# A hybrid encoder step on one core: squares turned by VectorE, an output projection two tiles ahead, and a sync queue in source order

## The chip, the core and the metric

The kernel runs on one core of one Trainium2 chip, in one launch. The metric is the device time of an execution in microseconds. Engines are named as the profile names them: PE is TensorE (PEld its weight loads), DVE is VectorE, ACT is ScalarE, POOL is GpSimd; SPq and ACTq are the instruction queues of SyncE and ScalarE that issue transfers.

## What is computed

One step of a two-layer encoder over 2048 prompt rows and 32 sampled rows of width 1024, all in float32. The first layer is a gated delta rule with 8 heads of 128; the second is a sliding-window attention with 16 query heads of 64, 4 key heads and a sink in each softmax. Both end in an output projection, a residual and a layer norm.

```python
def delta_layer(x, conv_buf, s0, w_in, conv_w, a_log, dt_bias, norm_w, w_out, ln_g, ln_b):
    proj = x @ w_in
    qkv, new_buf = causal_conv(proj[..., :CONV_DIM], conv_buf, conv_w)
    z = proj[..., CONV_DIM:CONV_DIM + A_VW].reshape(b, l, A_HEADS, A_DV)
    ...
    q = l2norm(qkv[..., :A_QK].reshape(b, l, A_HEADS, A_DK)) * (A_DK ** -0.5)
    k = l2norm(qkv[..., A_QK:2 * A_QK].reshape(b, l, A_HEADS, A_DK))
    v = qkv[..., 2 * A_QK:].reshape(b, l, A_HEADS, A_DV).astype(jnp.float32)
    ...
    o, s_new = gated_delta_rule(q, k, v, g, beta, s0.astype(jnp.float32))
    o = o * lax.rsqrt(jnp.mean(o * o, -1, keepdims=True) + RMS_EPS) * norm_w * jax.nn.silu(z.astype(jnp.float32))
    out = o.reshape(b, l, A_VW).astype(x.dtype) @ w_out
    return layer_norm(DN_ALPHA * x + out, ln_g, ln_b), new_buf, s_new.astype(x.dtype)
```

Behind it stand the shared key and value projection (`shared_kv`, a rotary turn on 16 of the 64 key dimensions) and the attention layer (`swa_layer`: own query and gate projections, banded softmax over 192 keys, output projection, layer norm). Outputs are y of all rows, the two states, the convolution rows and the last keys and values.

## The kernel before, in words

Every float32 product is split into a high and a low part and made of three products in a faster type, accumulated in PSUM. Five parts follow one another, with some overlap; intermediate tensors go through scratch in HBM.

**Projections (class P1, 0 to about 735 us).** Activations of all 2080 rows stay in SBUF in five blocks of 416. For each of 24 heads of q, k and v (indices 0 to 23), a row R of 128 channels by 2080 tokens is made by 5 x 24 products (`project`, lines 74 to 83). `conv` (line 199) then runs four taps, a tanh and a gate on it, and stores y, channels on partitions, to scratch in pieces of 512 bytes (lines 217 to 220). For q and k it squares y into the single buffer th on ScalarE, turns the squares in 32 x 32 squares on VectorE (line 225) and sums them for the norms. From head 15 on (`ordered`, line 232) the order of every engine is written by hand, with the decay matrices (`decays`) between. `split_out_weights` splits the output weights in 16 steps, one a head for heads 6 to 14, the others later. Then come 8 heads of the gate z.

**Delta rule (class Delta, about 710 to 1132 us).** 17 chunks: the 32 sampled rows first (chunk 0), then 16 of 128 rows. `ORDER` (line 613) is one list of steps with offsets: in iteration i the step `gq1+2` runs for chunk i+2, and so on, so that several chunks are under way at once. The list is the order of PE, DVE and ACT; the sync queue is ordered by a planner, which estimates when each transfer can start. Steps that matter here: `tk` and `tv` transpose keys and values on TensorE against the identity (`turn`, line 815), ScalarE scales the results out of PSUM (`kd`, `vn`; line 825), `fk` fades k in place after its transposes have been read, `Lk`, `Lv`, `Lq`, `Lz`, `Lgb`, `LE` are loads. k has two buffers. Up to iteration 10 the last gate products (`GA0` to `GA3`, class LateGate) fill TensorE; from iteration 11 the first layer's output weights are loaded in 16 steps. The sampled chunk makes its o early, but its gate and store come in `first_end` (line 1012), called at the last chunk's step `OSC`; `done` marks a chunk as stored.

**Output projection (classes OutNorm and O1).** 17 tiles in the order of their rows, the 32 sampled ones last. `O1.tiles` (line 1238) is a generator. In the last two iterations of the delta rule each TensorE step gives it 0.45 us of work (line 1003), afterwards it runs alone. For a tile it loads the gated o (g, one buffer) and the residual rows r one tile ahead, splits g in high and low parts, makes 2 x 24 products of 512 columns, adds them to r (line 1134), takes mean and variance and norms r in four half-row steps on VectorE (lines 1203 and 1205). `turned` (line 1224) then transposes the normed tile on TensorE, eight squares through PSUM, and stores it as hT. Between tiles `more` brings work of the next part: block 0 of hT (`load0`), and sums of blocks for a fast matrix product (`presum`, on GpSimd, stored from the sync queue, line 1376).

**Second layer's projections (class P2, about 1310 to 1735 us)** make keys, values, queries and gates, with seven products in place of eight for pairs of blocks (Strassen's scheme). `turn` (line 1710) transposes values on TensorE through one PSUM bank and two copies on ScalarE. `out_weights` splits the second layer's output weights beside it.

**Attention (class Attention, to the end)** isn't touched.

## Time and profile before

| | us |
|---|---|
| runs | 2104.82, 2105.94, 2102.75; median 2104.82 |
| profiled execution | 2110.58 |
| its span, first to last instruction | 2108.8 |
| mean granted TensorE clock | 0.989 |
| busy: PE, DVE, ACT, POOL | 2048.6, 1468.9, 989.0, 911.0 |

The span is what the traces below are measured in; the execution's own time has 1.8 us around it. A table of stretches gives for each engine the busy time and the number of instructions, then the granted clock, the mean share of the 16 transfer engines that were busy, and the bytes that they moved. A row of a timeline gives start, length, engine, line, operation and tiles, and in brackets how long the engine had stood idle and what ended that. A row of the groups by line gives count, busy time, mean length in ns, and idle time before.

### The profile page before, as it was taken

To read this page: it belongs to the slowest core of one execution; us is meant where nothing else is said; L and a number is where in the kernel's file an instruction comes from. 1 tells how busy PE (TensorE), PEld (TensorE's weight loads), DVE (VectorE), ACT (ScalarE), POOL (GpSimd) and SP (SyncE) were. 2 spreads that over 40 slices of the span, in tenths; PEclk is the share of its full clock that TensorE was granted. 3 is DMA by queue.
4 is the path that set the end of the run, shared out by engine and by line. 5 is a ranking of instruction groups with operands and counts; after the bars stand their busy time and mean duration, and the time that the engine had idled before them with its cause. 6 is when DMAs were issued, how large, how long until landed. Compare 5 with 4: busy or idle time off the path is not lost.

```text
span 2108.8 us, 37301 instructions
## 1 busy us (share of the span) xinstructions
PE 2048.6 (97%) x13694; PEld 1875.4 (89%) x13694; DVE 1468.9 (70%) x2587; ACT 989.0 (47%) x2465; POOL 911.0 (43%) x1248
## 2 busy tenths in 40 slices
PE   7999999999999999999999999999999999999998
PEld 5999999999999999999887887889989997777775
DVE  4476666675647678888887887768877755566565
ACT  4354444446532267777762211534644445455552
POOL 0322223212222177778752112157436515566666
PEclk9999999999999999999999999999999999999999
DMA  5132333236665545455766666778776659533421
GB/s 206 33 90 88 97 110 111 82 102 226 193 185 179 182 137 179 159 169 182 271 209 227 212 213 219 254 229 296 243 240 222 226 171 317 127 101 107 114 72 66
DMA packets 292763, 360.85 MB, mean 171 GB/s; under 512 B 74260, under 2 KB 217460, under 8 KB 292564
## 3 DMA queue, kind: packets, MB, share of 16 engines
q1 hardware_dynamic: 278576, 334.29, 49.9%
q10 hardware_dynamic: 14004, 24.17, 3.6%
q8 instruction: 108, 1.77, 0.3%
q14 instruction: 75, 0.61, 0.1%
HBM read 235.54 MB, written 134.06 MB: 175 GB/s over the span
## 4 chain that ended last, share of the span: by engine, by line
PE 83%; DMA 7%; DVE 3%; POOL 3%; issue 2%; ACT 1%; SPq 0%; ACTq 0%; DVEq 0%; POOLq 0%
PE ps L79 12%; PE ps L81 11%; PE ps L80 11%; PE ot L1126 3%; PE ot L1127 3%; PE ot L1128 3%; PE S L1992 2%; PE po L1126 2%; PE ot L2025 2%; PE po L1128 2%; PE po L1127 2%; PE tr L2007 2%; PE X L1653 2%; PE X L1651 2%; PE X L1652 2%
## 5 line engine op out<-in xcount | busy, mean ns | idle before, releaser
L79 PE MATMUL ps<-act_hi,w_hi 128*128 128x416 f32 x1280 | 454.9, 355 | 0.0
L81 PE MATMUL ps<-act_hi,w_lo 128*128 128x416 f32 x1280 | 450.2, 352 | 0.0
L80 PE MATMUL ps<-act_lo,w_hi 128*128 128x416 f32 x1280 | 447.9, 350 | 0.0
L79 PEld LDWEIGHTS ps<-act_hi,w_hi 128*128 128x128 f32 x1280 | 240.3, 188 | 3.8 <-issue 0.4
L80 PEld LDWEIGHTS ps<-act_lo,w_hi 128*128 128x128 f32 x1280 | 240.6, 188 | 3.0
L81 PEld LDWEIGHTS ps<-act_hi,w_lo 128*128 128x128 f32 x1280 | 240.1, 188 | 3.3
L209 DVE SCALAR_TENSOR_TENSOR y<-R,convw,y 128x2083 f32<-128x2083 f32 x72 | 182.5, 2536 | 60.9 <-ACT y L206 44.9
L56 POOL TENSOR_TENSOR w_lo<-w_raw,w_hi 128x1024 fp32r<-128x1024 f32 x25 | 71.4, 2858 | 330.9 <-ACT w_hi L55 303.6
L729 POOL TENSOR_TENSOR tm<-L,Tt 128x60 f32<-128x60 f32 (+19 forms) x365 | 132.5, 363 | 84.8 <-issue 39.9
L1826 POOL TENSOR_TENSOR P<-e,sm 128x384 f32<-128x384 f32 (+2 forms) x128 | 102.3, 820 | 118.0 <-DVE sm L1816 111.6
L731 POOL TENSOR_TENSOR Tt<-Tt,tm 128x60 f32<-128x60 f32 (+19 forms) x365 | 139.8, 383 | 28.6
L1812 ACT ACTIVATE e<-S,nm 128x193 f32<-128x193 f32 (+2 forms) x260 | 104.6, 415 | 97.3 <-DVE nm L1807 56.5
L1330 DVE TENSOR_TENSOR w_lo<-w_raw,w_hi 128x512 fp32r<-128x512 f32 x132 | 136.7, 1053 | 18.5 <-ACT w_hi L1342 12.7
L1126 PE MATMUL po<-wo_hi,g_hi 128*128 128x512 f32 x256 | 104.9, 410 | 8.1 <-DVE r L1134 7.9
L305 ACT COPY R<-ps 128x416 f32<-128x416 f32 (+1 forms) x144 | 60.4, 442 | 109.3 <-PE ps L81 95.8
L1482 ACT ACTIVATE o<-X 128x416 f32<-128x416 f32 x80 | 41.4, 518 | 134.7 <-PE X L1653 134.6
L1126 PE MATMUL ot<-wo,g_hi 128*128 128x512 f32 x256 | 103.6, 405 | 0.0
L1128 PE MATMUL po<-wo_hi,g_lo 128*128 128x512 f32 x256 | 101.2, 396 | 0.5 <-DVE g_lo L1169 0.5
L1127 PE MATMUL po<-wo_lo,g_hi 128*128 128x512 f32 x256 | 101.1, 395 | 0.0
L1127 PE MATMUL ot<-wo,g_hi 128*128 128x512 f32 x256 | 100.8, 394 | 0.0
L1128 PE MATMUL ot<-wo,g_lo 128*128 128x512 f32 x256 | 100.8, 394 | 0.0
L1342 ACT CAST w_hi<-w_raw 128x512 fp32r<-128x512 f32 x129 | 76.8, 616 | 21.5 <-PE ps L1652 6.7
(362 smaller groups left out, 5119.4 us busy)
## 6 DMA issues: line engine op xcount, KB each, us to landing
w_raw<-in_b_w SPq DMA_DIRECT2D x60, 512.0 KB
w_raw<-in_w_in SPq DMA_DIRECT2D x40, 512.0 KB
act_raw<-s_hT SPq DMA_DIRECT2D x64, 208.0 KB
s_rows<-o SPq DMA_DIRECT2D x50, 208.0 KB
k<-s_k SPq DMA_DIRECT2D x17, 512.0 KB
E<-s_E SPq DMA_DIRECT2D x17, 512.0 KB
s_bq<-s_rows SPq DMA_DIRECT2D x40, 208.0 KB
s_bz<-o SPq DMA_DIRECT2D x40, 208.0 KB
```

Source lines behind the costliest of these rows:

```text
L79: nc.tensor.matmul(ps, hi[:, k, :], xh[:, k, :], start=(k == 0), stop=False)
L80: nc.tensor.matmul(ps, hi[:, k, :], xl[:, k, :], start=False, stop=False)
L81: nc.tensor.matmul(ps, lo[:, k, :], xh[:, k, :], start=False, stop=(k == KC - 1))
L209: nc.vector.scalar_tensor_tensor(out=y[:], in0=R[:, j:j + W], scalar=self.convw[:, i, j:j + 1], in1=y[:], op0=ALU.mult, op1=ALU.add)
L729: P.tensor_tensor(out=tm[:n, i0 - k:, :w], in0=L[:n, i0:, j:j + 1].to_broadcast(sh), in1=Tt[:n, j:j + 1, :w].to_broadcast(sh), op=ALU.mult)
L731: P.tensor_tensor(out=Tt[:n, i0:, :w], in0=Tt[:n, i0:, :w], in1=tm[:n, i0 - k:, :w], op=ALU.subtract)
L1126: nc.tensor.matmul(ps[:n], ghi[:, k, :n], hi, start=a, stop=False)
L1127: nc.tensor.matmul(ps[:n], ghi[:, k, :n], lo, start=False, stop=False)
L1128: nc.tensor.matmul(ps[:n], glo[:, k, :n], hi, start=False, stop=z)
L1330: P.tensor_tensor(out=lo, in0=raw, in1=hi, op=ALU.subtract)
L1812: self.nc.scalar.activation(x.e[:, h, u, :x.n], x.S[:, h, u, :], AF.Exp, bias=x.nm[:, h, u:u + 1], scale=1.0, accum_out=x.sm[:, h, u:u + 1])
L1826: self.nc.gpsimd.tensor_tensor(out=x.P[:, u, :nj * 128].rearrange("r (j h k) -> r j h k", h=2, k=64), in0=x.e[:, :, u, :n].rearrange("r h ...
```

## The change

It does four things.

- Keys and values are turned in the first stage. For k and v, VectorE turns y itself in 32 x 32 squares; for k the squares are taken afterwards, so the number of turns is the same, and for v they are added. `by_token` stores the turned tile to scratch with tokens on rows, in pieces of 32 floats, four transfers a head for the prompt and four for the sampled rows. The delta rule loads them so (`Lt`, `Lv`) and ScalarE scales them in place; `tk` and `tv` go. The loads have new places in `ORDER`.
- The output projection's normed rows and the second layer's values are turned by VectorE in squares too, and stored in pieces of 32 floats.
- `O1.tiles` is rewritten: g comes two tiles ahead, the norm of a tile ends during the next one (a scaling on ScalarE, two full-row products and a turn on VectorE), the sampled tile is first and waits for its gate, which is made after the last chunk's store. `load0` and the presums are spread over tiles, and the presums are stored from ScalarE's queue.
- The sync queue takes the source order in the delta rule, and in the projection ScalarE and the sync queue do.

Besides, the first layer's output weights are split at heads 1 to 6, and the second layer's begin eight steps later.

```diff
@@ P1.qkv
-            if 6 <= i < self.FREE:
+            if 1 <= i < 7:
                 next(self.wo)
@@ P1.conv
+        if kind < 2:
+            dst = T["qk"[kind]]
...
+        pieces = (th[:, 0:NP], y[:, 0:NP]), (th[:, NP:NT], y[:, NP + 3:NP + 3 + NS])
+        if kind == 0:
+            for a, b in pieces:
+                nc.scalar.activation(a, b, AF.Square)
+            nc.vector.transpose(R[:, 0:NT], th[:, 0:NT])
+        else:
+            for a, b in pieces:
+                nc.vector.transpose(a, b)
+            self.by_token(T[("kt", "v")[kind - 1]], h, th)
+            if kind == 2:
+                return
+            yield
+            nc.scalar.activation(R[:, 0:NT], th[:, 0:NT], AF.Square)
...
+    def by_token(self, dst, h, turned):
+        for a in range(4):
+            s = slice(32 * a, 32 * a + 32)
+            self.nc.sync.dma_start(dst[0:NTT - 1, :, h, s].rearrange("t (b i) j -> i (t b) j", i=32),
+                                   turned[s, 0:NP].rearrange("i (b j) -> i b j", j=32))
+            self.nc.sync.dma_start(dst[NTT - 1, 0:NS, h, s], turned[s, NP:NT])
@@ Delta
-        ta2+0 fq1+1 os0+0 v5+0 Lk+2 PC2+1 OSC+-1 Lq1+2 PC3+1 fq0+1 vn0+1 G0+2 u3+0 N0+2 G1+2 TT+2 otr0+-1
...
+        at0+2 o1+0 y1+1 ks0+1 e0+1 U32+1 ks1+1 Lk+3 v2+1 v3+1 GA2+1 gth+0 sq1+0 Lv0+2 Lv1+2 WL+1 X+0
+        Lz1+0 Lq0+3 ta1+1 v4+1 gz1+0 GA0+2 u1+1 e1+1 R+0 gz2+0
...
+    def by_token(self, ch, q, src, dst):
+        t = self.four.tile([128, 4, 128], F32, tag=dst, name=dst)
+        ch.__dict__.setdefault(dst, {})[q] = t
+        self.nc.sync.dma_start(t[:ch.n], self.T[src][ch.ti, :ch.n, q * 4:q * 4 + 4, :])
...
-    def turn(self, ch, x, name):
-        tr = self.bank(self.pa, ch, name)
-        for j in range(4):
-            self.nc.tensor.transpose(tr[:ch.n, j, :], x[:, j, :ch.n], self.G["ident"][:, :])
...
                     if c == last and name == "OSC":
-                        self.first_end(chunks[0], second, done)
+                        second.give(5.5)
                     if name == "st1":
                         done(chunks[c])
+                        if c == last:
+                            self.first_end(chunks[0], done)
+                            second.give(1.5)
@@ OutNorm
+    def scaled(self, r, n):
...
+        V.tensor_scalar(out=nb[:n], in0=mv[:n, 0:1], scalar1=rs[:n, 0:1], scalar2=-1.0, op0=ALU.mult, op1=ALU.mult)
+        nc.scalar.activation(r[:n], r[:n], AF.Identity, bias=nb[:n, 0:1], scale=rs[:n, 0:1])
+
+    def affine(self, r, n):
+        V, tabs = self.nc.vector, self.tabs
+        V.tensor_tensor(out=r[:n], in0=r[:n], in1=tabs[0][:n], op=ALU.mult)
+        V.tensor_tensor(out=r[:n], in0=r[:n], in1=tabs[1][:n], op=ALU.add)
@@ O1.turned
+        hT = self.room().rearrange("p a b -> p (a b)")
+        self.nc.vector.transpose(hT[:n], h[:n])
+        self.nc.sync.dma_start(self.T["h"][row:row + n, :], h[:n])
+        rows = self.T["hT"].rearrange("h (c j) t -> j (h c) t", j=32)
+        for a in range(0, n, 32):
+            self.nc.sync.dma_start(rows[:, :, c0 + a:c0 + a + 32],
+                                   hT[a:a + 32].rearrange("j (c i) -> j c i", i=32))
@@ O1.tiles
+        on, last, parts, beside = self.on, None, [], ()
+        for t in tiles[:2]:
+            while not ready(t):
+                yield 1.0
+            g = self.fetch(*t)
+            yield 0.0
+            parts.append(on.low(g, on.cast(g, t[2]), t[2]))
         r = self.rows(*tiles[0])
         for i, t in enumerate(tiles):
+            beside, coming = itertools.chain(beside, more(i)), tiles[i + 2:i + 3]
+            if i + 1 == len(tiles):
+                yield from (out for out in beside if out)
+            for j, out in enumerate(on.tile(parts.pop(0), r, t[2])):
+                yield out
+                if j == 0:
+                    for c in coming:
+                        while not ready(c):
+                            yield 1.0
+                        g = self.fetch(*c)
+                next(beside, None)
+                if j == 1 and last:
+                    on.affine(*last)
+                    self.turned(last[0], *tiles[i - 1])
+                if j == 3 and i + 1 < len(tiles):
+                    following = self.rows(*tiles[i + 1])
+            for c in coming:
+                high = on.cast(g, c[2])
+            on.scaled(r, t[2])
+            for c in coming:
+                parts.append(on.low(g, high, c[2]))
+            last, r = (r, t[2]), following
+        on.affine(*last)
+        self.turned(last[0], *tiles[-1])
+        yield from more(len(tiles))
@@ P2.out_weights
+        for _ in range(8):
+            yield
@@ P2.turn
+        nc, t = self.nc, self.out()
+        nc.vector.transpose(t[:], c[:])
...
+        for a in range(4):
+            self.delay(lambda a=a: store(a), 1 + a)
@@ program
-        tiles = [(t * 128, t * 128, min(128, NT - t * 128)) for t in range(NTT)]
+        tiles = [(t * 128, t * 128, min(128, NT - t * 128)) for t in (NTT - 1, *range(NTT - 1))]
         yield from o1[0].tiles(tiles, lambda t: t[0] in sent, more)
 
     def more(i):
+        if 6 <= i < 10:
+            yield from p2[0].load0(2 * i - 12)
+        elif 12 <= i < 16:
+            for _ in range(4 if i < 15 else 0):
+                next(p2[0].main)
+            yield from p2[0].presum(0, p2[0].raw_act, 2, (i - 12,), nc.scalar, 3)
+        elif i == 16:
+            yield from p2[0].go(4)
+        elif i == 17:
+            yield from p2[0].go(8)
...
-    with tc.manual_schedule(engines={ET.PE, ET.DVE, ET.Activation}):
+    with tc.manual_schedule(engines={ET.PE, ET.DVE, ET.Activation, ET.SP}):
         delta.run(chunks, S, LateGate(p1, zp, w, raw), second, side, done)
...
-    with tc.manual_schedule(engines={ET.PE}):
-        with tc.manual_schedule(engines={ET.DVE}):
-            second.rest()
+    with tc.manual_schedule(engines={ET.PE, ET.DVE, ET.Activation, ET.SP}):
+        second.rest()
```

## Rows read from the trace of the kernel before

**Rows 1.** The page's first part: busy time, share of the span and instructions.

```profile
PE 2048.6 (97%) x13694; PEld 1875.4 (89%) x13694; DVE 1468.9 (70%) x2587; ACT 989.0 (47%) x2465; POOL 911.0 (43%) x1248
```

**Rows 2.** Busy time of each engine by stretch of the span.

```profile
core 0: us, PE busy (x) PEld busy (x) DVE busy (x) ACT busy (x) POOL busy (x), PEclk, DMA share, GB/s
...
250.00:430.00 180.00, 180.00 (x958) 178.36 (x957) 119.37 (x50) 76.77 (x94) 43.83 (x46) 1.00 0.32 100
...
735.00:980.00 245.00, 245.00 (x2760) 233.13 (x2759) 202.34 (x486) 172.33 (x556) 185.80 (x496) 0.99 0.49 162
980.00:1081.00 101.00, 92.98 (x1184) 89.32 (x1182) 89.96 (x245) 74.19 (x252) 78.58 (x221) 0.98 0.73 246
...
1132.00:1332.00 200.00, 192.10 (x906) 158.09 (x904) 157.12 (x337) 33.71 (x50) 41.91 (x35) 0.98 0.67 218
1332.00:1735.00 403.00, 389.19 (x2023) 378.29 (x2022) 294.46 (x375) 187.97 (x380) 196.65 (x127) 0.97 0.73 237
```

**Rows 3.** Groups by line, engine PE: the transposes; count, busy us, mean ns, idle.

```profile
L818 PE MATMUL vtr<-ident,v 128*128 128x128 f32 (+1 forms) x136 | 21.8, 283 | 0.0
...
L1232 PE MATMUL ps<-ident,r 128*128 128x128 f32 (+1 forms) x132 | 19.4, 269 | 0.2 <-ACT o L1439 0.2
...
L818 PE MATMUL ktr<-ident,k 128*128 128x128 f32 (+1 forms) x136 | 17.9, 274 | 0.2 <-DVE npr L702 0.2
...
L1714 PE MATMUL tp<-ident,o 128*104 128x128 f32 x40 | 7.0, 303 | 3.2 <-ACT o L1718 3.2
```

**Rows 4.** Timeline of PE in the steady delta rule.

```profile
836.28 1.03 PE L818 MATMUL ktr<-ident,k 128*128 128x128 f32 x8
837.15 1.06 PE L846 MATMUL vp<-vn,u 128*128 128x128 f32 x8
```

**Rows 5.** The chain that ended last: start us, us, what; pieces of chunks, two loads.

```profile
846.65 1.09 PE gq L831 x8
...
870.44 1.09 PE gq L831 x8
...
965.59 1.09 PE gq L831 x8
...
1011.67 6.43 DMA k<-s_k
...
1074.52 1.09 PE gq L831 x8
...
1249.93 2.44 DMA act_raw<-s_hT
```

**Rows 6.** Waits of PE and DVE: us in total, times, longest us.

```profile
PE po L1126 <- DVE r L1134: 7.9, 3, 3.8
...
PE tp L1714 <- ACT o L1718: 3.2, 2, 3.0
...
DVE k L841 <- PE ktr L818: 13.5, 13, 1.4
```

**Rows 7.** Timeline of DVE in the output projection.

```profile
1208.29 0.69 DVE L1234 COPY hT<-ps 128x512 f32<-128x512 f32 x1 [1.91 <-PE ps L1232]
...
1215.66 1.22 DVE L1169 TENSOR_TENSOR g_lo<-g,g_hi 128x1024 fp32r<-128x1024 f32 x1
...
1220.12 0.69 DVE L1234 COPY hT<-ps 128x512 f32<-128x512 f32 x1 [1.91 <-PE ps L1232]
```

**Rows 8.** Line 225, DVE: the turn of squares; ns min, median, max.

```profile
L225 DVE STREAM_TRANSPOSE R<-th x16: 2285/2345/2346, 98.9 to 421.9; 128x2080 f32<-128x2080 f32 x16
```

**Rows 9.** Groups of PE from 1081 to 1132 us: the projection's products.

```profile
L1126 PE MATMUL po<-wo_hi,g_hi 128*128 128x512 f32 x32 | 13.6, 426 | 0.2 <-ACT g_hi L1168 0.2
```

**Rows 10.** Stretches with stores of 512-byte pieces, then 128-byte pieces; columns as [rows 2].

```profile
262.30:266.20 3.90, 3.90 (x22) 3.87 (x22) 2.29 (x1) 2.01 (x3) 0.00 (x0) 1.00 0.98 273
...
1334.10:1334.90 0.80, 0.80 (x6) 0.78 (x5) 0.69 (x2) 0.00 (x0) 0.00 (x0) 1.00 1.11 174
```

More of the change, by code (lines that the diff above doesn't have):

```diff
@@ L1015, in first_end @@
         self.load(c0, "z")
-        second.give(5.5)
         for q in range(2):
@@ L1021, in first_end @@
         done(c0)
-        second.give(1.5)
     def sampled(self, pool):
@@ L1179, in tile @@
             cs = slice(c * 512, c * 512 + 512)
[L1180 removed]
+            ps = self.bank(c)
             for k in range(KC):
@@ L1213, in __init__ @@
         self.on = OutNorm(tc, es, "o1", "left", I, "a", 2, T["wo"])
-        self.bank = lambda: self.on.pp.tile([128, 512], F32, tag="po", name="tr")
-        self.steps = 0
-        self.room = lambda: self.on.one.tile([128, KC, 128], F32, tag="g", name="hT")
+        self.steps, self.room = 0, None
     def fetch(self, c0, row, n):
@@ L1253, in tiles @@
-            while not all(ready(u) for u in tiles[i + 1:i + 2]):
-                yield 1.0
-            ahead = self.fetch(*tiles[i + 1]) if i + 1 < len(tiles) else None
-            following = self.rows(*tiles[i + 1]) if i + 1 < len(tiles) else None
-            self.on.queue = self.nc.sync if i < 9 else self.nc.scalar
-            for j, out in enumerate(self.on.tile(got, r, t[2], True)):
-                if isinstance(out, float):
-                    yield out
-                    if j == 3 and ahead is not None:
-                        ahead = self.on.split(ahead, tiles[i + 1][2])
-                    if j >= 6:
-                        yield from itertools.islice(late, 1)
@@ L1265, in tiles @@
-            self.nc.sync.dma_start(self.T["h"][t[1]:t[1] + t[2], :], out[:t[2]])
-            late = self.turned(out, *t)
-            got, r = ahead, following
-            if i + 2 == len(tiles):
-                yield from more(1)
-        yield from more(2)
-        yield from late
+            beside, coming = itertools.chain(beside, more(i)), tiles[i + 2:i + 3]
[14 more added lines that the diff above has]
+                    following = self.rows(*tiles[i + 1])
@@ L1359, in take_act, with presum @@
         return t
-    def presum(self, pair, load, pace, slices=range(4)):
+    def presum(self, pair, load, pace, slices=range(4), queue=None, hold=0):
         c, d = self.PAIRS[pair]
@@ L1374, in presum @@
                     yield
+            for _ in range(hold):
+                yield
             for n, t in (("t1", b11), ("t3", b12), ("t2", b22), ("t4", b21)):
-                self.nc.sync.dma_start(T["sums"][pair, int(n[1]) - 1, k], t[:])
+                (queue or self.nc.sync).dma_start(T["sums"][pair, int(n[1]) - 1, k], t[:])
                 for _ in range(pace // 4):
@@ L1710, in turn, with store @@
     def turn(self, c, half, b):
[L1711 to L1719 removed]
+        nc, t = self.nc, self.out()
+        nc.vector.transpose(t[:], c[:])
+        rows = self.T["bv"][b * TB:(b + 1) * TB, half * 128:half * 128 + 128]
+        rows = rows.rearrange("(b i) (a j) -> a i b j", i=32, j=32)
+        def store(a):
+            s = slice(32 * a, 32 * a + 32)
+            nc.sync.dma_start(rows[a], t[s].rearrange("i (b j) -> i b j", j=32))
+        for a in range(4):
+            self.delay(lambda a=a: store(a), 1 + a)
 class Attention:
@@ L2283, in side @@
             o1.append(O1(tc, left, I, O, T, G))
+            o1[0].room = lambda: delta.four.tile([128, KC, 128], F32, tag="k", name="hT", bufs=Delta.BUFS)[:]
         else:
```

153 lines of the change are left out of this document (53 added, 100 removed).

## The prediction, made before the changed kernel ran

> **What bounds the kernel now.** I read the shares of busy time first, then the table by stage, then the groups of TensorE, then timelines and chain. TensorE is busy 97% of the span [rows 1]; the reader should see that it is the only engine near full. The table by stage [rows 2] shows where: it has no gap in the projections (250 to 430 us) and in the steady part of the delta rule (735 to 980), with VectorE at 202.3 of 245 us there. It has gaps where the delta rule runs without gate products (980 to 1081: 93.0 of 101), in the output projection (1132 to 1332: 192.1 of 200) and in the second layer's projections (1332 to 1735: 389.2 of 403). So in the gapless stretches a TensorE instruction that goes is time that goes; in the others I have to look for what ends the gap.
>
> **The transposes on TensorE.** There are 136 + 136 for keys and values, 136 of the normed rows (132 and a group of 4) and 40 of the second layer's values [rows 3]. Their durations of some 270 ns overlap; the price is start to start: eight key transposes begin at 836.28 and the next product at 837.15, so 0.87 us, 0.109 us each [rows 4]. All 448 are 48.8 us if TensorE bounds everywhere. It doesn't, so part by part:
>
> *Delta rule, steady.* A full chunk has 16 transposes, 16 x 0.109 = 1.74 us. The period is 870.44 - 846.65 = 23.79 us [rows 5], without a gap; it would be 22.05. VectorE needs 202.3/245 x 23.79 = 19.6 us of it and fits. VectorE also loses its wait for the key transposes before the fading of k, 13.5 us over 13 chunks [rows 6]; ScalarE scales as many tiles as before, from loaded tiles. I take 1.6 of the 1.74 us for ten chunks: **16 us** (ends: 0 and 17).
>
> *Delta rule, last chunks.* From 965.59 to 1074.52 five periods take 21.8 us each [rows 5], with TensorE idle; VectorE is busy 90.0 of 101 us [rows 2], 19.4 us a period, and the load of k holds the chain for 6.43 us [rows 5]. The change issues that load in the iteration before, once its buffer is free. VectorE then sets the period; with 1 us of waits that stay I take 20.4, so 5 x 1.4 = **7 us** (ends: 2, and 5 x 1.74 = 9). The first two chunks give **2 us**.
>
> *Output projection, steady.* A tile takes 1220.12 - 1208.29 = 11.83 us [rows 7], with 8 transposes, 0.87 us. On VectorE goes a copy (0.69) and four half-row steps of about that (2.8); to it come two full-row products at 1.22 (the full-row subtraction in the same rows) and one turn of 1024 columns, half of 2.345 us for 2080 [rows 8], 1.15: 3.6 against 3.5 us. It waited 1.91 us a tile for the transposes [rows 7], so it fits into 10.96 us. Saved: 136 x 0.109 = 14.8 us, and TensorE's wait for r (7.9 us [rows 6]), since r and g now come a tile earlier and the presums' stores leave the sync queue for ScalarE's. The granted clock of the stretch is 0.98 [rows 2]; without those waits some 4 us of half-clock time come back. Together 26.7.
>
> *Output projection, its start.* Here the change costs. It puts the sampled tile first and waits for it, but that tile's gate is only made after the last chunk is stored. So nothing of the projection can run beside the last chunks any more. Before, 96 products (three groups of 32, [rows 9]) ran there, at about 0.23 us each: 22 us. Without them the stretch 1081 to 1132 can't shrink by all of it, for the last chunk is a chain through three engines; I take 19, a loss of 3. Then TensorE stands still while o of the sampled rows is loaded, turned, gated, stored and loaded again as g: three transfers in a row, at 2.44 us each [rows 5], with issues, a cast and a subtraction 12 us. After it I allow 2 us at the lower clock. **-17 us**; with transfers of 6.43 us [rows 5] -29, with a chain that hides half -8. I take the quiet value, since the loads of the weights are over by then. The projection nets 26.7 - 17 = **10 us**.
>
> *Second layer.* 40 x 0.109 = 4.4 us, and TensorE's wait for the copies out of the one turning bank, 3.2 us [rows 6], go; ten turns of 416 columns (0.47 us) come to VectorE, which is busy 294 of 403 us [rows 2]. Weights now fetched and cast during the last tiles, and output weights that start eight steps later, take perhaps 2 of the 13.8 us of gaps. **9.6 us** (ends 4 and 14).
>
> *First stage: costed at nothing, and why.* VectorE gets eight turns more (v), 8 x 2.345 = 19 us; TensorE's gapless row covers it, with VectorE busy 119 of 180 us [rows 2]. The turned tile is stored in pieces of 128 bytes, 8192 a head against 2048 of 512. The price of a piece: a store of the 512-byte kind moves 273 GB/s at share 0.98, so 17.4 GB/s an engine, 29 ns a piece; the sampled rows' store of hT, in 128-byte pieces, moves 174 GB/s at 1.11 (transfers that begin in the stretch count whole), 13 ns [rows 10]. A head is 120 products at 180/958 us, 22.5 us [rows 2]; its pieces take 8192 x 13/16 = 6.7 us of all engines, so a share of 0.30 on top of 0.32. That fits. The single buffer of th is now read by these stores, and the next head's tanh waits for it; it comes some 16 us later, and behind it ScalarE's copies can be late by several banks before TensorE notices. The page "DMA: Bandwidth & Descriptors" of the Trainium skill (Specifications) puts line rate at 512 bytes or more and says that smaller transfers are read, modified and written. By that rule a piece would cost more than one of 512 bytes, and the sum would be the slower rival below; the trace so far shows it at under half.
>
> *Sync queue.* In source order each load waits behind those before it. They are placed where their buffers come free; the tightest are the values, issued after the squares that free their tiles, some 4 us of TensorE work before ScalarE scales them. At 2.44 us they are in time, at 6.43 us they hold ScalarE, and behind it the copies that the next products need, by 2 to 3 us. I take nothing, since the nearest load by size (208 KB against 256) took 2.44.
>
> **The sum.** 16 + 7 + 2 + 10 + 9.6 = 45 us off the profiled execution's 2110.58 (its span is 2108.8): 2065.6. The median of the runs, 2104.82, lies 5.8 us under that execution: **2060**.
>
> **Rivals.** *VectorE becomes the bound.* For it: in [rows 2] it is at 83 to 89% in the delta rule, and its order is fixed, so waits don't pack. Against it: the waits it loses. The steady chunks then give 0.8 us (8), the last ones 3, and tiles stay near 11.4 us, so 8 of the projection's gain go: 45 - 8 - 4 - 8 = 25 less, 2080. *The start of the projection costs little and the second layer's gaps close:* 9 more from the start, 8 from the gaps, 5 of clock: 2038. *The sync queue in order makes it slower.* One mechanism: the values' loads come late in each chunk. It decides once a load takes over some 4 us; by 3 us over, 15 chunks lose 45 us and the gain is gone (2105); at 4 us it is 2120. For it: the 6.43 us load; against it: that one ran beside the load of the 8 MB of output weights. *Small pieces fill the transfer engines in the first stage.* The point is (1 - 0.32) x 22.5 x 16/8192 = 30 ns a piece; at 40 ns a head's pieces take 20.5 us, with the rest 27.7 against 22.5, 16 heads lose 83 us: 2143. By the Trainium skill's rule named above it is this one that comes; the 13 ns of [rows 10] speak against it. *That a part of the change does nothing:* fetching two tiles ahead can't help while the first tile waits; that is in the forecast already.
>
> **The numbers.** 0.2% is 4.2 us, about what a measurement can tell. Forecast 0.52 (2042 to 2076), VectorE 0.2, the better case 0.13, the sync queue 0.1 (half of it within 0.2% or just faster), small pieces 0.05. Faster 0.85, same 0.04, slower 0.11. The range reaches to the first two rivals and their bounds, 2032 to 2094, and leaves out both slow cases and the edge of the good one.
>
> **What would show it.** The steady period at 22.0 to 22.2 us; the wait of k for key transposes gone; no projection product before the last turn of o, then 10 to 14 us without TensorE; tiles at 11.0 us; no waits of the projection for r; the share of the transfers at 0.6 in 250 to 430 us with TensorE gapless. I would be wrong if the period stays over 23 us, if TensorE shows gaps before 700 us, or if the stand at the start of the projection is over 20 us.

## The result, and the profile after

The changed kernel takes 2110.95 us (median of 10 executions, 2107.54 to 2120.86); the kernel before, on the same chip, 2103.05. The ratio is 1.0039 (95% interval 1.0022 to 1.0057): 8 us slower. 2060 was forecast, with a range of 2032 to 2094, so the time lies outside it on the far side.

The busy shares, which answer to [rows 1]:

```profile
PE 2011.6 (95%) x13246; PEld 1838.5 (87%) x13246; DVE 1493.6 (71%) x2604; ACT 1001.2 (47%) x2437; POOL 904.3 (43%) x1248
```

TensorE is busy 37 us less than before and the span is the same (2108.3 against 2108.8): the work left, and idle time came in its place. The same stretches as in [rows 2], of the kernel after, show where:

```profile
core 0: us, PE busy (x) PEld busy (x) DVE busy (x) ACT busy (x) POOL busy (x), PEclk, DMA share, GB/s
...
250.00:430.00 180.00, 180.00 (x953) 178.18 (x952) 112.44 (x58) 72.91 (x79) 32.22 (x39) 1.00 0.53 116
...
735.00:980.00 245.00, 241.60 (x2665) 228.37 (x2662) 206.66 (x499) 181.76 (x576) 188.46 (x505) 0.97 0.61 199
980.00:1081.00 101.00, 87.28 (x1109) 81.34 (x1108) 91.88 (x243) 75.65 (x245) 81.99 (x219) 0.98 0.82 279
1081.00:1132.00 51.00, 31.02 (x272) 24.86 (x271) 21.49 (x71) 17.12 (x61) 2.01 (x7) 0.77 0.27 75
1132.00:1332.00 200.00, 192.69 (x840) 160.14 (x839) 171.84 (x341) 48.48 (x54) 41.60 (x32) 0.97 0.83 224
1332.00:1735.00 403.00, 383.51 (x1994) 374.32 (x1994) 300.20 (x384) 181.19 (x361) 202.48 (x131) 0.99 0.77 245
```

Read the first row first: the first stage is gapless with the small pieces in it. Then 1081 to 1132: TensorE stands 20 of 51 us, at a clock of 0.77. The waits of TensorE, kernel after, in order of size (answering to [rows 6]):

```profile
PE ps L1682 <- DVE w_lo L1354: 11.4, 3, 6.1
PE y1p L793 <- DVE tcp L769: 11.4, 10, 2.5
PE otr L941 <- ACT u L836: 6.8, 7, 1.6
PE po L1140 <- DVE g_hi L1195: 6.2, 1, 6.2
PE otr L941 <- DVE o L932: 5.7, 1, 5.7
PE ps L1680 <- DVE r L1151: 4.8, 1, 4.8
...
PE otr L941 <- DMA os<-s_o: 3.9, 1, 3.9
...
PE ps L1143 <- DVE r L1151: 2.6, 1, 2.6
```

The start of the projection is three of these in a row, in the timeline of TensorE, kernel after:

```profile
1111.01 1.97 PE L941 MATMUL otr<-ident,o 128*128 128x128 f32 x8 [5.66 <-DVE o L932]
1116.89 1.03 PE L941 MATMUL otr<-ident,os 32*128 32x32 f32 x8 [3.91 <-DMA os<-s_o]
1124.10 0.69 PE L1140 MATMUL po<-wo_hi,g_hi 128*64 128x512 f32 x1 [6.18 <-DVE g_hi L1195]
1124.58 0.63 PE L1141 MATMUL po<-wo_lo,g_hi 128*32 128x512 f32 x1
...
1130.11 0.39 PE L1140 MATMUL po<-wo_hi,g_hi 128*64 128x512 f32 x1
1130.33 0.40 PE L1141 MATMUL po<-wo_lo,g_hi 128*32 128x512 f32 x1
```

That is 15.8 us without work, and then products 0.43 us apart at the lower of the clock's two levels instead of 0.23. The end of the projection is held by r; the chain that ended last, kernel after, from 1300 to 1325 us, has it like this:

```profile
1304.15 1.02 SPq L1253
...
1305.22 3.60 SPq L1253
...
1308.86 5.19 DMA s_hT<-hT
...
1314.06 6.11 DMA r<-in_x
...
1320.25 0.70 DVE r L1151
```

L1253 is the store of the turned rows in 128-byte pieces. Between it and the load of r the sync queue (timeline, kernel after) issued four loads for the second layer:

```profile
1303.50 6.05 SPq L1253 DMA_DIRECT2D s_hT<-hT  x4
1309.60 4.18 SPq L1338 DMA_DIRECT2D act_raw<-s_hT  x4
1314.06 0.33 SPq L1178 DMA_DIRECT2D r<-in_x  x1
```

Between 1295 and 1400 us TensorE waits 7.4 us for r (2.6 and 4.8) and once 6.1 for `w_lo`, the low part of the second layer's weights; the kernel before waits for neither longer than 0.9 us there.

The same journey as five legs, bounded by the starts of named TensorE products in each trace (first `ks`, the product of state and keys, of the delta rule; last turn of o; last projection product; first scores of attention; end of span), in us:

| kernel | to first ks | delta rule | projection | second layer to first scores | rest |
|---|---|---|---|---|---|
| before | 731.0 | 401.3 | 189.6 | 412.3 | 374.6 |
| after | 734.4 | 383.2 | 199.6 | 415.7 | 375.4 |
| e1 row order | 736.5 | 409.2 | 164.3 | 419.0 | 375.1 |
| e2 planner in the rest | 735.2 | 380.6 | 198.5 | 408.8 | 375.7 |
| e3 planner everywhere | 733.3 | 376.4 | 204.0 | 405.7 | 375.9 |
| e4 first stages alone | 731.4 | 391.5 | 190.8 | 409.8 | 374.2 |
| e5 row order, planner | 734.6 | 400.9 | 166.8 | 411.2 | 374.8 |
| e6 last turn alone | 730.1 | 400.6 | 186.7 | 408.7 | 374.0 |
| f1 first stages and last turn | 733.9 | 386.1 | 188.6 | 405.7 | 374.9 |
| g1 source order, 512-byte stores | 734.9 | 381.1 | 194.9 | 403.1 | 375.6 |

Kernels that run projection products beside the last chunks pay for them in the third column and save them in the fourth: those two are read as a sum. From before to after the delta rule wins 18, the projection loses 10, and the legs before and behind lose 3 each. One execution's legs carry some us of chance: the profiled execution of before lay 7.5 us above its median, that of after 0.8 below. So the ledger that follows uses ratios to the kernel before of the same comparison (0.001 is 2.1 us), and the legs only to say where.

### The profile page after: what moved, and what is told of

It reads as the page before. It is cut to its first block, busy times and chain, and to the rows that moved or that the text cites. A ratio compares the mean times of both kernels' runs of the same rounds, so it can differ in the third digit from the quotient of the medians.

```text
span 2108.3 us, 36624 instructions
## 1 busy us (share of the span) xinstructions
PE 2011.6 (95%) x13246; PEld 1838.5 (87%) x13246; DVE 1493.6 (71%) x2604; ACT 1001.2 (47%) x2437; POOL 904.3 (43%) x1248
## 5 line engine op out<-in xcount | busy, mean ns | idle before, releaser
L209 DVE SCALAR_TENSOR_TENSOR y<-R,convw,y 128x2083 f32<-128x2083 f32 x72 | 175.1, 2434 | 54.5 <-ACT y L206 43.5
L215 DVE SCALAR_TENSOR_TENSOR y<-th,y 128x2083 f32<-128x2083 f32 x24 | 55.8, 2326 | 31.5 <-ACT th L213 31.5
L1396 POOL TENSOR_TENSOR act_raw<-act_raw 128x416 f32<-128x416 f32 x32 | 44.7, 1396 | 66.8 <-DMA act_raw<-s_hT 65.5
L1839 DVE TENSOR_REDUCE nm<-S 128x4 f32<-128x772 f32 (+3 forms) x66 | 60.6, 918 | 16.5 <-PE S L2024 16.4
```

The lines of the kernel that those rows point to most:

```text
L209: nc.vector.scalar_tensor_tensor(out=y[:], in0=R[:, j:j + W], scalar=self.convw[:, i, j:j + 1], in1=y[:], op0=ALU.mult, op1=ALU.add)
```

## The experiments

### What each part does alone

**e4**: the kernel before, with only the first three stages changed; **e6**: with only `turn` and its second PSUM bank; **f1**: both. In e4 and f1 the sync queue stays with the planner until the second layer.

```diff
-            self.nc.tensor.transpose(tr[:ch.n, j, :], x[:, j, :ch.n], self.G["ident"][:, :])
...
+        self.nc.sync.dma_start(t[:ch.n], self.T[src][ch.ti, :ch.n, q * 4:q * 4 + 4, :])
```

for e4, and for e6:

```diff
-            nc.tensor.transpose(tp[:w, j, :], c[:, j * w:j * w + w], self.ident[:, :])
...
+        nc.vector.transpose(t[:], c[:])
```

> The kernel before with only the first three stages changed (keys and values turned by VectorE, loaded by token, the delta rule's new order), its sync queue left to the planner; the projection and the second layer as before. Theory A (the delta rule gains, and what comes behind it gives the gain away): delta rule 383 to 386 us from the first key state to the last turn of o against 401.3, nothing lost behind it, 2103 - 16 = 2087 (2083 to 2092). Rival B (the gain of the delta rule itself is lost again whatever follows, because the projection's products then lack cover under the last chunks): 2097 to 2104.

> The kernel before with only the second layer's values turned by VectorE (40 transposes off TensorE, 128-byte stores from the sync queue). Theory A (the prediction's 4.4 us of transposes and 3.2 us of wait): the stretch from the projection's last product to the first scores falls from 412.3 to 404 to 408 us, and the time by 4 to 8 us, to 2097 to 2101. Rival B (the 128-byte stores in the hand-written sync order hold back the weights' loads behind them): no change or up to 5 us slower, 2104 to 2110.

> The kernel before with the first three stages changed and the second layer's values turned by VectorE; the projection as before, sync queue planned up to the second layer. It leaves out the whole rewrite of the projection. Theory A (the two parts add, 0.9973 and 0.9966, and the rewritten projection, even in row order, was worth next to nothing): ratio 0.994, the same as the run in row order with the planner (e5, 0.9938). Rival B (the two parts share the same idle time and don't add): 0.9965 to 0.998, and the rewritten projection is then worth 6 to 9 us in row order.

Measured: e4 0.9973 (0.9958 to 0.9989), 5.7 us faster; e6 0.9966 (0.9954 to 0.9978), 7.2 us; f1 0.9955 (0.9935 to 0.9975), 9.5 us. The last turn does what was forecast. The first stages do not: 16 was expected here, 25 in the prediction. Eight steady periods of e4 take 180.4 us, 22.55 each against 23.79, but the last six take 137.4 against 133.5. The row of 950 to 1080 us of e4 (columns as [rows 2]):

```profile
950.00:1080.00 130.00, 112.68 (x1351) 105.20 (x1350) 110.24 (x291) 92.97 (x302) 97.86 (x269) 0.95 0.73 250
```

and the largest wait of TensorE in e4 from 953 to 1140 us:

```profile
PE g L718 <- DMA k<-s_k: 10.0, 5, 2.5
```

TensorE is idle for 17 of 130 us and its clock is 0.95 there; k comes late to five of the last chunks. This goes with the planner: in every run that has the new stages and a planned sync queue in the delta rule, the wait for k between 953 and 1140 us is 5.8 to 10.5 us over five chunks, in every run with that queue in source order 1.1 to 3.1 (8.5 against 2.5 in e3 and e2 below, which differ in this alone). The six periods take 132.2 us in f1, which has the same stages, so the 137.4 are in part this execution's chance. By its time, 2098.16 us, e4 falls to its rival B. f1 against e4 and e6 shows that the two parts add within the intervals (0.0061 in sum, 0.0045 together).

### The start of the projection

**e1**: the changed kernel with the tiles in row order, so that their products can run beside the last chunks; **e5**: the same with the sampled rows' step back at its old place and the sync queue planned.

```diff
-        tiles = [(t * 128, t * 128, min(128, NT - t * 128)) for t in (NTT - 1, *range(NTT - 1))]
+        tiles = [(t * 128, t * 128, min(128, NT - t * 128)) for t in range(NTT)]
```

> The changed kernel with the projection's tiles in row order again, the sampled tile last, so that its products can fill the end of the delta rule. Theory A (the late start is what the change lost most by): from the last turn of o to the projection's last product 199.6 us becomes 178 to 184, the three waits of 3.9 to 6.4 us between 1105 and 1124 are filled with products, and the time falls from 2111 to 2091 to 2096. Rival B (the end of the delta rule is bound by VectorE and its chain, so products laid beside it make it longer by what they bring): 2107 to 2112, the last turn of o 10 us or more later than 1117.6. Rival C (the second layer is bound by transfers, and every earlier end of the projection turns into a longer wait there): the projection ends earlier, but the first product of the second layer that reads the last operands stays near 1360, and the time is 2107 to 2111.

> The changed kernel with the tiles in row order, the sampled rows' step back at its old place (beside the last chunk's end) and the sync queue left to the planner in both parts. Theory A (late start and source order are two separate losses): first key state to the projection's last product 565 to 572 us against 580.4 of the run with the planner alone (e3), and what follows unchanged (406 and 376), so 2099 - 10 = 2089 (2085 to 2093). Rival B (what the projection gains at its start is lost again in the second layer, as in the run in row order alone, where 9.3 us were won and 3.3 lost): 2095 to 2100.

Measured: e1 0.9994 (0.998 to 1.0009), against 1.0039 of the changed kernel; e5 0.9938 (0.9922 to 0.9954), against 0.9983 of e3. Both steps are 0.0045, 9.5 us: late start and source order are separate losses, and e5 is the version that beats both kernels, 2090.53 us, 13 us under the one before. In e1 less came than theory A wanted (2106.1 us): delta rule and projection together are 9.3 us shorter than after, the second layer's leg 3.3 longer, as rival C had it in small.

### The sync queue

**e2**: the changed kernel with the projection's rest planned; **e3**: the delta rule too; **e8**: source order kept, the load of r directly behind the rows' store.

```diff
-    with tc.manual_schedule(engines={ET.PE, ET.DVE, ET.Activation, ET.SP}):
+    with tc.manual_schedule(engines={ET.PE, ET.DVE, ET.Activation}):
         second.rest()
```

and for e8:

```diff
-        self.nc.sync.dma_start(self.T["h"][row:row + n, :], h[:n])
...
+                    self.nc.sync.dma_start(self.T["h"][tiles[i - 1][1]:tiles[i - 1][1] + last[1], :], last[0][:last[1]])
+                    if i + 1 < len(tiles):
+                        following = self.rows(*tiles[i + 1])
                     self.turned(last[0], *tiles[i - 1])
-                if j == 3 and i + 1 < len(tiles):
+                elif j == 1:
                     following = self.rows(*tiles[i + 1])
...
```

> The changed kernel with the sync queue of the projection's rest left to the planner instead of source order; the delta rule's sync queue stays in source order. Theory A (at the end of the projection the load of r stands behind eight loads and stores that source order puts ahead of it): the waits for r of 2.6 and 4.8 us before 1322 go, the stretch from the last product of the projection to the steady second layer shrinks from 43 to 30 to 35 us, and the time is 2099 to 2104. Rival B (the transfer engines are simply full there, share 0.9 to 1.0, and any order pays): within 3 us of 2111.

> As the run before, and the delta rule's sync queue left to the planner too. Theory A (source order does neither good nor harm in the delta rule, as the prediction costed it): within 3 us of the run before. Rival B (loads in source order hold ScalarE in the delta rule, and that is why a period took 22.5 us instead of 22.05): period 22.1, 5 to 8 us faster than the run before. Rival C (the planner issues the loads later than their written places): periods of 23 us and more, 5 to 15 us slower.

> The changed kernel, source order kept in the sync queue, but the load of the next tile's r is issued right behind the store of the rows, ahead of the four 128-byte stores and of the loads for the second layer. Theory A (in source order r comes too late, and that is the projection's loss at its end): the waits of 2.6 and 4.8 us for r are gone, the time is 4 to 8 us under 2111. Rival B (r is not the point; the loads and casts for the second layer are what comes late): the waits for r go, but the 6 us wait for w_lo at 1341 grows by as much, and the time is within 3 us of 2111. Rival C (the load of r now holds the stores behind it until the rows are stored): 2 to 6 us slower than 2111.

Measured: e2 0.9986 (0.997 to 1.0002), 11 us under the changed kernel; e3 0.9983 (0.9966 to 1.0), the same again; e8 1.0113 (1.0093 to 1.0133), 16 us over it. So source order costs 11 us, all of it behind the delta rule, and r alone is not the cure: in e8 the load waits for the rows' store, and the queue waits with it. Timeline of the sync queue in e8:

```profile
1304.83 0.71 SPq L1280 DMA_DIRECT2D s_h<-r  x1
1310.88 0.33 SPq L1178 DMA_DIRECT2D r<-in_x  x1
1311.27 3.87 SPq L1252 DMA_DIRECT2D s_hT<-hT  x4
```

and TensorE's longest wait in e8, at the projection's end:

```profile
PE ps L1683 <- DVE r L1151: 12.8, 1, 12.8
```

The store was issued at 1304.83 and the load only at 1310.88, when the store had landed. Theory A falls, rival C is right and was too small. In e2 and e3 the waits for r are gone, and the one for `w_lo` behind them falls from 6.1 us to 1.5 and 0.5.

### The 128-byte stores

**f3** (on e5) and **g1** (on the changed kernel): each full tile's rows stored as they lie, in one transfer of 1024 pieces of 512 bytes in place of four of 1024 pieces of 128. They leave out the last part of the turn, so the second layer's input is not the right one. **g2**, **h1**: the four stores issued by ScalarE's and GpSimd's queue; **g4**, **h2**: the same on e5.

```diff
-        for a in range(0, n, 32):
-            self.nc.sync.dma_start(rows[:, :, c0 + a:c0 + a + 32],
-                                   hT[a:a + 32].rearrange("j (c i) -> j c i", i=32))
...
+            self.nc.sync.dma_start(self.T["hT"][:, :, c0:c0 + n].rearrange("h p t -> p h t"),
+                                   hT.rearrange("p (h t) -> p h t", t=128))
```

for f3 and g1; in g2 and g4 only `nc.sync` becomes `nc.scalar`, in h1 and h2 `nc.gpsimd`.

> As e5, but the turned rows of the full tiles are stored as they lie, in one transfer of 512-byte pieces in place of four of 128-byte pieces. It leaves out the last part of the turn (each square's columns don't go to their own rows), so that what the second layer computes is not the reference's. Theory A (the small pieces fill the transfer engines at the end of the projection and hold up the loads and stores there): from the projection's last product to the second layer's steady part 38 us becomes 28 to 32 and the time 2080 to 2085. Rival B (the pieces cost little, the loads of weights and sums are what fills the engines): within 3 us of e5.

> The changed kernel as it is, source order kept, but the turned rows of a full tile stored as they lie in one transfer of 512-byte pieces in place of four of 128-byte pieces (it leaves out the last part of the turn, so that what the second layer computes is not the reference's). Theory A (source order costs 11 us because each tile's four stores hold the queue 5 to 6 us, and r and the operands stand behind them): most of the 11 us come back, 2098 to 2103, with the waits for r of 2.6 and 4.8 us gone. Rival B (what costs is the order itself: loads of the second layer's operands ahead of r, whatever the stores take): within 4 us of 2111. The pieces alone were worth 5 us in row order with the planner (f3 against e5), so 2106 would leave it between them.

> The changed kernel with the four 128-byte stores of a tile issued by ScalarE's queue in place of the sync queue; nothing else moved. Theory A (the slow issues of these stores on the sync queue are the loss): 2100 to 2106. Rival B (ScalarE, which also casts g and the weights and stores the sums, is then held by the same 5 us a tile, and the loss only moves): 2108 to 2118.

> The changed kernel with the four 128-byte stores of a tile issued by GpSimd's queue, which has little to do in the projection; nothing else moved. Theory A (an in-order queue that loads or computes stands behind the 5 to 6 us of issues; ScalarE's was no better a place, but GpSimd's is idle): most of what 512-byte pieces gave comes back, 2096 to 2103. Rival B (the 4096 pieces themselves fill the transfer engines, whoever issues them): within 4 us of 2111.

> As e5 (row order, planner), the 128-byte stores issued by ScalarE's queue. Theory A (the sync queue's issues hold up the second layer's first loads): 2 to 5 us faster than e5. Rival B (ScalarE pays them): 0 to 8 us slower.

> As e5 (row order, planner), the 128-byte stores issued by GpSimd's queue. Theory A: 3 to 6 us faster than e5 (2090.5), near the 2085 of 512-byte pieces. Rival B: within 3 us of e5, or slower as GpSimd's sums for the second layer come later.

Measured: f3 0.9908 (0.9886 to 0.993), 6 us under e5; g1 0.9952 (0.9934 to 0.997), **18 us under the changed kernel with the order untouched**; g2 1.0031 (1.0016 to 1.0045), no gain; h1 0.9978 (0.9966 to 0.999), 13 us under the changed kernel; g4 0.9982 (0.9969 to 0.9995), 9 us over e5; h2 0.9952 (0.9936 to 0.9969), no better than e5. In g1 no wait for r is left and 0.5 us for `w_lo` at the second layer's start, in place of 6.1. The issues themselves by line of source (ns: least, median, most), in the changed kernel:

```profile
L1253 SPq DMA_DIRECT2D s_hT<-hT x65: 303/693/4262, 1144.9 to 1333.6; - x65
```

in g1, one transfer a tile:

```profile
L1255 SPq DMA_DIRECT2D s_hT<-hT x16: 370/371/377, 1153.6 to 1321.6; - x16
```

and in h1, on GpSimd:

```profile
L1253 POOL DMA_DIRECT2D s_hT<-hT x65: 783/783/957, 1148.0 to 1338.2; - x65
```

In g1 the sync queue gets from store to r in 5 us (its timeline):

```profile
1297.94 0.37 SPq L1255 DMA_DIRECT2D s_hT<-hT  x1
1298.37 4.85 SPq L1340 DMA_DIRECT2D act_raw<-s_hT  x4
1303.27 0.76 SPq L1178 DMA_DIRECT2D r<-in_x  x1
```

Four loads still stand ahead of r and take 4.85 us to issue, but r goes out at 1303.27 in place of 1314.06, for a projection that ends 6 us earlier. So with stores of 512-byte pieces the order is harmless: g1 lies 0.0044 over f3, and the late start alone is 0.0045. With stores that hold their queue for 3.0 to 3.8 us a tile at first and 5.3 to 7.2 us near the end it is not.

Of the 18 us, 11 come back when the planner orders the queue (e2) and 13 when GpSimd's queue issues the stores (h1). How they divide between the issuing queue and the pieces in the transfer engines is not shown, since h1 moved more than the issues. Its page lists GpSimd's stores in few large packets (queue and kind: packets, MB, share of 16 engines):

```profile
q0 software_dynamic: 3120, 8.52, 2.1%
```

These are 2.7 KB each, and the engines' share from 1120 to 1280 us falls from 0.75 in the changed kernel to 0.68, toward the 0.64 of g1. The 6 us of f3 against e5, where the planner had already moved the loads past the stores, speak for a price in the engines; that h2, at a share of 0.75 against 0.84 in e5, gains nothing speaks against it. On ScalarE's queue the loss only moves (TensorE then waits 10.3 us for `w_hi`, cast by ScalarE).

### TensorE's transposes of the normed rows

**e7**, **f2**: e5 with the normed rows turned by TensorE, at the second and at the seventh of a tile's eight steps.

```diff
-        self.nc.vector.transpose(hT[:n], h[:n])
...
+                nc.tensor.transpose(tr[:, j, :n], h[:n, k * 128:k * 128 + 128], self.G["ident"][:n, :n])
```

and in f2 beside it

```diff
-                    self.turned(last[0], *tiles[i - 1])
-                if j == 3 and i + 1 < len(tiles):
+                if j == 6 and last:
+                    self.turned(last[0], *tiles[i - 1])
+                if j == 7 and i + 1 < len(tiles):
```

> As the run in row order with the planner (e5), but the normed rows are again turned by TensorE, copied by ScalarE and VectorE and stored in 512-byte pieces. Theory A (TensorE is the bound in the projection's steady part, and a tile's eight transposes cost 0.87 us): about 15 us slower than e5, tiles of 11.8 us. Rival B (the 128-byte stores cost as much as the transposes, on the sync queue and on the transfer engines at the end of the projection): within 4 us of e5. Between them: the tiles' 13 to 15 us come back in part, as the second layer's start gets its loads earlier: 5 to 9 us slower.

> As e5 (row order, planner), with the normed rows turned by TensorE again and stored in 512-byte pieces, but now at the seventh of a tile's eight steps, so that the rows are finished when TensorE reaches them (in e7 it waited 5.8 us a tile for them). Theory A (TensorE bounds the projection; eight transposes are 0.87 us a tile): 10 to 15 us slower than e5, so 2100 to 2106. Rival B (the 128-byte stores give back what the transposes cost, through the transfers at the end of the projection): within 4 us of e5.

Measured: e7 1.0665, f2 0.9985 (0.9968 to 1.0001). e7 tells nothing of its theories: TensorE reaches the transposes before the rows are finished and stands 99.1 us in 17 waits. f2 is 0.0047, 10 us, over e5. Its tiles take 11.77 us (transposes at 1165.20, 1176.97, 1188.75), those of e5 10.83 (VectorE's turn at 1149.13 and, nine tiles on, at 1246.63), so the steady gain is there, and near the 0.87 forecast; but one wait of 9.3 us for the last rows at 1320 is f2's own, and the ends of the two delta rules differ by 6 us. The 10 us are a sum of these and no clean price. Against f3, which stores 512-byte pieces as f2 does, it is 0.0077, 16 us, with the same reserve.

### Two that settled little

**f4**: e5 with the second layer's first operands one tile earlier. **g3**: e5 with the first stage's turned tiles stored in 512-byte pieces.

```diff
-        if 6 <= i < 10:
-            yield from p2[0].load0(2 * i - 12)
-        elif 12 <= i < 16:
+        if 5 <= i < 9:
+            yield from p2[0].load0(2 * i - 10)
+        elif 11 <= i < 15:
...
```

for f4, and for g3, which leaves out the last part of the turn of keys and values:

```diff
-            self.nc.sync.dma_start(dst[0:NTT - 1, :, h, s].rearrange("t (b i) j -> i (t b) j", i=32),
-                                   turned[s, 0:NP].rearrange("i (b j) -> i b j", j=32))
...
+        self.nc.sync.dma_start(dst[0:NTT - 1, :, h, :].rearrange("t p k -> p t k"),
+                               turned[:, 0:NP].rearrange("p (t k) -> p t k", k=128))
```

> As e5, with the second layer's first operands and presums started one tile earlier, which row order allows. Theory A (the end of the projection is crowded by transfers, and spreading them by 11 us takes some of the crowd away): 2 to 6 us faster than e5. Rival B (they then crowd the tile before, and nothing changes): within 2 us of e5.

> As e5, but the turned keys and values of the first stage are stored as they lie, in pieces of 512 bytes in one transfer a head (it leaves out the last part of the turn, so that the delta rule's result is not the reference's). Theory A (the prediction's: the first stage pays nothing for its 128-byte pieces): the first key state stays at 732 to 736 us and the time within 3 us of e5. Rival B (the pieces, at a share of 0.5 to 0.8, make the stage some 3 us longer): first key state at 731, 3 us or more faster than e5.

Measured: f4 0.9948 (0.9929 to 0.9967), within the intervals the same as e5; g3 0.9955 (0.9938 to 0.9972), first `ks` at 736.2: not faster, so no price of the pieces in the first stage shows, though 3 us either way would hide in the intervals. That its end moved from 730.1 and 731.0 (the two kernels with the old stage) to between 731.4 and 738.3 (the others) has another cause, which stays open.

## Why the prediction was wrong, point by point

The ledger from the ratios, in us: first stages and last turn -9.5 (f1), the projection's rewrite in row order -3.6 (e5 against f1), its late start +9.5 (e3 against e5), source order with 128-byte stores +11.8 (after against e3); together +8.2. The steps are a chain of kernels from before to after, so they must add up to the result; what each is worth would differ in another order. The prediction had -34.6, -26.7, +17 and 0. The two losses decide the sign, and they were 4 us larger than forecast in sum. The gains were 48 us smaller: that is where most of the miss lies. So these steps failed: the projection's steady gain (26.7 put, 3.6 measured), the first stages and last turn (34.6 put, 9.5 measured), and the sync queue, put at nothing, which cost 11.8 and turned a small gain into a loss. By step:

**"Output projection, steady ... Together 26.7"** measured 3.6, inside the intervals of the two runs. The tile itself came out as forecast (10.96): VectorE's turns in the changed kernel, at 1196.93, 1207.81 and 1218.69, are 10.88 us apart. From the 193rd of the 800 products (four full tiles in) to the last e5 takes 142.5 us and f1 157.0: there the gain is had. Three things took it back. The delta rule's end is less well filled: its leg is 14.8 us longer in e5 than in f1, for 112 products beside it in place of 96, of which the 16 more explain 3.7 (16 x 0.23); one wait of 5.4 us for o before a turn stands there that f1 doesn't have, but f1 has one of 5.3 for r, so the cause of the rest stays open. The second layer's leg is 5.5 us longer; TensorE's waits there explain 2 of it (17.5 us from 1295 to 1735 against 15.3), and the granted clock is 0.98 against 0.99. And "TensorE's wait for r (7.9 us), since r and g now come a tile earlier" did not go: 2.6 and 4.8 us are left in the changed kernel. Only g comes a tile earlier; r keeps two buffers, so its load must follow the store of the rows before. Nor did the 4 us of half-clock time come back: the median granted clock of the executions is 0.992 for the kernel before, 0.989 for f1, 0.984 for e5 and 0.983 for the changed kernel.

**Delta rule, steady, "1.6 of the 1.74 us"** measured 1.25 a chunk (eight periods of 22.55 us in e4, 22.52 in the changed kernel). TensorE's work fell as forecast, from 23.8 to 22.17 us a period, but in every second period it now waits for VectorE. Two neighbouring periods of the changed kernel:

```profile
893.30:916.50 23.20, 22.18 (x258) 21.18 (x257) 20.70 (x51) 16.82 (x55) 19.28 (x51) 1.00 0.58 193
916.50:938.80 22.30, 22.16 (x258) 21.18 (x258) 19.57 (x50) 16.89 (x55) 18.38 (x51) 1.00 0.62 199
```

and the only wait of TensorE in the first of them:

```profile
PE y1p L793 <- DVE tcp L769: 1.0, 1, 1.0
```

**Delta rule, last chunks, "7 us"**: without the projection's products beside them, in the changed kernel, they gained 5.8 (127.7 us for six periods against 133.5); with them they lost 3.9 in e4 and gained 1.3 in f1. The "1 us of waits that stay" held for k, where the changed kernel's source order brings it in time, but other waits took its place. The waits of TensorE from 953 to 1140 us, kernel after:

```profile
PE y1p L793 <- DVE tcp L769: 9.4, 6, 2.5
PE otr L941 <- ACT u L836: 6.2, 6, 1.6
...
PE g L718 <- DMA k<-s_k: 1.1, 1, 1.1
```

So the step had the load of k right; it took VectorE by its busy time and left out the waits in the chain through VectorE and ScalarE.

**"Sync queue ... I take nothing"** was 11 us. The step weighed one place, the values' loads in the delta rule, and rightly found nothing there (e2 against e3: 0.0003). It did not follow the queue to the end of the projection, where in source order each tile's four stores and the second layer's loads stand ahead of r. The change also put all loads of r on that queue, which its description and the prediction both pass over. Before, ScalarE's queue issued those of the last tiles (ns: least, median, most), first the kernel before, then after:

```profile
L1161 ACTq DMA_DIRECT2D r<-in_x x8: 332/339/455, 1079.6 to 1310.0; - x8
L1178 SPq DMA_DIRECT2D r<-in_x x17: 333/614/2481, 1124.5 to 1314.1; - x17
```

No run puts them back, so how much of the 11 us that alone would save stays open. The rival that made the queue the cause had the right kind of loss in the wrong place; that its 2105 to 2120 hold the measured time is luck.

**The price of a 128-byte piece was used for the first stage alone.** It held there: gapless at a share of 0.53 (0.6 was forecast). In the projection the prediction left out the 4096 pieces a tile and their issues. Their engine time can be read from 1120 to 1280 us, first the changed kernel (columns as [rows 2]):

```profile
1120.00:1280.00 160.00, 155.91 (x675) 125.74 (x676) 135.41 (x268) 36.57 (x39) 14.62 (x12) 0.97 0.75 200
```

then g1:

```profile
1120.00:1280.00 160.00, 157.55 (x683) 127.16 (x684) 138.26 (x280) 37.63 (x39) 14.67 (x13) 0.97 0.64 209
```

A share of 0.11 over 160 us and 16 engines is 282 us, 19 a tile (14.6 tiles of 10.96 us); with 1024 x 29 ns of the 512-byte store, as the prediction had it, that makes, by estimate, 49 us for 4096 pieces, 12 ns each, beside its 13 from [rows 10]. The page "DMA: Bandwidth & Descriptors" of the Trainium skill (Specifications) puts pieces under 512 bytes below line rate. By bytes the runs agree: four pieces of 12 ns move what one of 29 moves. That a small piece costs more than a large one they do not show.

**The late start** was priced at 17 and measured 9.5 (e1 and e5 alike). Its mechanism was right: the changed kernel stands 15.8 us in three waits, 10.1 of them behind the turn of the last full chunk's o, where 10 to 14 were forecast, then works 6 us at half clock. The loss of 3 beneath the last chunks was nearer 1: the delta rule of e3 is 24.5 us shorter than that of e5 (376.4 against 400.9), for 112 products less, 26 us at 0.23. What the price left out is the second layer, which gives part of the loss back: its leg is 5.5 us shorter in e3 than in e5, and 3.3 shorter in the changed kernel than in e1. Why, the runs do not show.

**The second layer's 9.6** measured 7.2 alone (e6), within its ends of 4 and 14. In the changed kernel the start covers it: in place of the 2 us to be won from gaps there are 11.4 us of waits for `w_lo` (4.8 before) and 4.8 for r.

## What to carry to other kernels

Before adding up the work that a change takes off the bounding engine, follow each queue past every instruction that the change puts into it, to the stage behind. A store in many small pieces holds the queue that issues it, and in a queue kept in order everything behind it waits; a load put ahead of it helps only if the load itself need not wait, as it had to in e8. A tile that needs the end of a chain goes last, not first.

## What the runs showed of the hardware

The issue of a store of 1024 pieces took the sync queue 0.37 us with pieces of 512 bytes and a median of 0.69, at most 4.26, with pieces of 128 bytes; on GpSimd's queue 0.78 with hardly any spread, in packets of 2.7 KB on average. ScalarE, too, is held by issues: in g2, behind 5.5 us of these stores and 4.2 us of four stores of sums, its next cast began after 14.2 us of standing. And TensorE's products came 0.43 us apart for 6 us after a stand of 15.8 us in three parts, at a granted clock of 0.50, the lower of its two levels (1.2 GHz); from 1130.1 us on they came 0.23 apart, at 1.00.
